# A macaron encoder layer in fp32: column updates ahead of the lower parts of X^T, the token scale spread one chunk later, and the first loads in another order

## The chip, the cores and the metric

The kernel runs on one core of a Trainium2 chip. The time is the device time of one execution in microseconds; 1860.35 us is the median of three runs (1859.88 to 1862.2). The engines are named as the profile names them: PE is the matrix engine and PEld its weight loads, DVE the vector engine, ACT the scalar engine, POOL the GpSimd engine, SP the engine whose queue issues nearly all loads.

## The reference

One layer on 256 tokens of width 2048, all in float32; the feed-forward width is 5632.

```python
ff = swiglu(rms_norm(x, pre_norm_ffn1), w_ffn1_gate_up, w_ffn1_down)
x = x + 0.5 * rms_norm(ff, post_norm_ffn1)
h = rms_norm(x, pre_norm_mix)
q_h, i_h, f_fwd, f_bwd, g_h, q_a, k_a, v_a = split(h @ w_mix_in)
y_h = hgrn2_mixer(q_h, i_h, f_fwd, f_bwd, g_h, ...)   # gated linear recurrence, both ways
y_a = window_attention(q_a, k_a, v_a, attn_sink, rel_bias_table)
x = x + rms_norm(concat(y_h, y_a) @ w_mix_out, post_norm_mix)
ff = swiglu(rms_norm(x, pre_norm_ffn2), w_ffn2_gate_up, w_ffn2_down)
x = x + 0.5 * rms_norm(ff, post_norm_ffn2)

def rms_norm(x, gain): return x * rsqrt(mean(x * x, -1) + 1e-6) * gain
def swiglu(x, w_gate_up, w_down):
    gate, up = split(x @ w_gate_up); return (silu(gate) * up) @ w_down
```

The change touches the first feed-forward block's start, the normalisation of both feed-forward blocks, and the ends of the first feed-forward block and of the mixer, where `x` is updated and the next product begins.

## The kernel before

**Products.** Every fp32 operand is a sum of two parts: `h`, the value rounded by a cast on ACT (L176), and `l`, the rest, by a subtraction on DVE (L177). A product is three matmuls of 128x512 on PE: h with X's upper part, l with X's upper part, h with X's lower part. Weights come in raw tiles of 128x2048 (three buffers, `raw`), each cast in two halves of 128x1024 into `h` and `l` (five buffers each). A raw tile is one unit of a group, and `work(u)` of a group is the products of one unit.

**X^T.** X lies in rows of 128 tokens (m = 0, 1) and four quarters of 512 columns (q = 0 to 3). `turn(m, q)` (L210) makes four transposes on PE into one bank, of the pool `pa` for m = 0 and `pb` for m = 1. `take_hi` (L227) makes the upper part on ACT, times a gain, and `take_lo` (L232) the lower part on DVE. A step in the code named T(m, q) below is `turned(m, q)`.

**The start** is written by hand (`manual_schedule`): the instructions of every engine stand in the order of the code. X^T of the first quarter, the first unit in pieces, then T(0,1), T(1,1) and the units 1 and 2, with `busy` matmuls of no use between the first ones. Group 0 of the gate/up product runs on the raw X^T, without the token scale 1/rms.

**The token scale.** While group 0 runs, the sums of squares are made on ACT, and at unit 4 the scale is spread over all partitions: two diagonal matrices `dg` on DVE (L267), a product with ones on PE (L268), a copy into `R` (L269). Then eight multiplications on DVE (`even`, L818) scale X^T in place, a few a unit, and all later groups read the scaled X^T. In the first block the bias rows of the attention are made beside it (`aside`, L1000 and L1001).

**The ends.** `finish` (L588 to L726) runs the last held units of the down (or output) product bank by bank: (m, n) = (0,0), (0,1), (1,0), (1,1). After each bank come the squares on ACT (L569) and the products with the gain on DVE (`gains`, L576); after n = 1 the row's factor `r` (tot, v, then a power on POOL, L182 to L186). `update(m, q)` (L623) adds `y * r` to a quarter of X, and T(m, q) turns that quarter for the next product, whose first two units are the *lead*: `lead.pieces(m)` yields four pieces of it, and `lead.more(i)` casts one half of its second unit. Order on PE, DVE and ACT is the order of the code here too; elsewhere a scheduler orders. The last `finish` (no gain) is another branch.

Of the kernel before, what the change touches and what calls it, by code (L numbers as in the profile page):

```python
# [37 lines left out]
def hymba_layer_kernel(  # L38
# [53 lines left out]
    def load_x(m, q, n=1):  # L92
        sl = slice(q * 512, (q + n) * 512)
        nc.sync.dma_start(res["X"][:, m, sl], x[0, m * P : (m + 1) * P, sl])
# [31 lines left out]
    def busy(n):  # L126

        bank = pb()
        for i in range(n):
            nc.tensor.matmul(bank, idle[:, 0:P], idle, start=(i == 0), stop=(i == n - 1))  # L130
# [98 lines left out]
    def take_lo(*a):  # L229

        for src, g, hi, lo in take_views(*a):
            nc.vector.scalar_tensor_tensor(  # L232
                lo, src, g, hi.bitcast(F32), ALU.mult, ALU.subtract
            )
# [275 lines left out]
    class Pairs(Blocks):  # L510
# [62 lines left out]
        def gains(self, m, n, dst=None):  # L573
            if dst is None:
                dst = self.y[m, 2 * self.now + n]
            nc.vector.tensor_tensor(  # L576
                dst, self.c[m][n], self.pg[:, n * 512 : (n + 1) * 512], ALU.mult
            )
# [9 lines left out]
        def finish(self, mul, post, new_x=None, gain=None, lead=None):  # L588


            order = self.orders[1]
            n_order = len(order)
            self.post = post
            self.work(n_order - self.HELD)
            held = []
            for u in order[n_order - self.HELD :]:
                held.append((u, *split_load(self.source(u), hp=post, lp=post)))
            close_far()
            self.half_gain(post)
            if new_x:  # L600
                new_x()
            X = res["X"]
            if lead:
                lead.load()
            r = [None, None]
            y = self.y

            def products(m, n, part):
                for u, k, hs, ls in [
                    (u, k, hs, ls) for u, hs, ls in held for k in range(2)  # L610
                ][part]:
                    self.plain(u, hs, ls, m, n, k)

            def squares(m, n):
                self.squares(m, n)
                if n == 1:
                    r[m] = rsqrt_of(self.ssq[m], 1.0 / (D * mul * mul), EPS / (mul * mul))

            gains = self.gains

            def update(m, q):
                sl = slice(q * 512, (q + 1) * 512)
                nc.vector.scalar_tensor_tensor(  # L623
                    X[:, m, sl], y[m, q], r[m], X[:, m, sl], ALU.mult, ALU.add
                )

            def update_aside(m, q):
                sl = slice(q * 512, (q + 1) * 512)
                nc.scalar.mul(y[m, q], y[m, q], r[m])
                nc.gpsimd.tensor_tensor(X[:, m, sl], X[:, m, sl], y[m, q], ALU.add)  # L630

            ordered = {mybir.EngineType.PE, mybir.EngineType.DVE, mybir.EngineType.Activation}
            every = slice(None)
            if gain is None:
                def store(m, q):
                    sl = slice(q * 512, (q + 1) * 512)
                    nc.sync.dma_start(out[0, m * P : (m + 1) * P, sl], X[:, m, sl])

                def in_place(n):
                    gains(1, n, dst=self.c[1][n])  # L640
                    y[1, 2 + n] = self.c[1][n]

                with tc.manual_schedule(engines=ordered):
                    products(0, 0, every)
                    squares(0, 0)
                    gains(0, 0)
                    products(0, 1, every)
                    squares(0, 1)
                    gains(0, 1)
                    products(1, 0, every)  # L650
                    squares(1, 0)
                    for q in range(4):
                        update(0, q)
                    in_place(0)
                    products(1, 1, every)
                    squares(1, 1)
                    in_place(1)
                    for q in range(4):
                        store(0, q)
                    update_aside(1, 0)  # L660
                    for q in (1, 2, 3):
                        update(1, q)
                        store(1, q)
                    store(1, 0)
                return None

            xt = new_xt()

            banks = {}

            def turned(m, q):
                banks[m, q] = turn(m, q)

            def hi(m, q):
                take_hi(m, q, gain, xt, banks[m, q])

            def lo(m, q):
                take_lo(m, q, gain, xt, banks[m, q])

            with tc.manual_schedule(engines=ordered):  # L680
                products(0, 0, every)
                squares(0, 0)
                gains(0, 0)
                products(0, 1, every)
                squares(0, 1)
                update(0, 0)
                gains(0, 1)
                products(1, 0, every)
                lead.more(0)
                update(0, 1)  # L690
                squares(1, 0)
                gains(1, 0)
                products(1, 1, slice(0, 3))

                def took(m, q):
                    hi(m, q)
                    lo(m, q)

                turned(0, 0)
                took(0, 0)  # L700
                products(1, 1, slice(3, None))
                turned(0, 1)
                squares(1, 1)
                took(0, 1)
                update(1, 0)
                update(1, 1)
                lead.more(1)
                first, second = lead.pieces(0, xt), lead.pieces(1, xt)
                next(first)
                next(first)  # L710
                turned(1, 0)
                took(1, 0)
                gains(1, 1)
                next(first)
                turned(1, 1)
                took(1, 1)
                for _ in first:
                    pass
                for m, q in ((0, 2), (1, 2), (0, 3), (1, 3)):
                    update(m, q)  # L720
                    next(second)
                    turned(m, q)
                    took(m, q)
                for _ in second:
                    pass
            return xt  # L726

# [66 lines left out]
    def ffn(gated, w_dn, post_gain, again, gain=None, lead=None, aside=None):  # L794

        with ExitStack() as st:
# [74 lines left out]
            for g in range(NG):  # L871
                if g:
                    gated.group(g)
                for u in range(gated.pos, KT // 2):
                    gated.work(u + 1)
                    if g == 0:
                        if u == 4:
                            power_and_rest()
                            spread(two)
                        for done in {4: (0, 1, 2), 5: (3, 4), 6: (5, 6), 7: (7,)}.get(u, ()):  # L880
                            even(done)
                        if u == 5 and aside:
                            aside()
                    if waiting and u == 0:
                        next(waiting)
                waiting = units(gated.c, rest if g else rs2)
                next(waiting)
# [26 lines left out]
    with tc.manual_schedule():  # L914
# [12 lines left out]
        def arrive(i):  # L927
            nc.sync.dma_start(raw[:, i * 512 : (i + 1) * 512], first[:, i // 2, i % 2])
# [5 lines left out]
        def half(i):  # L934
            cs = slice(i * 512, (i + 1) * 512)
            split_act(h[:, cs], l[:, cs], raw[:, cs])
# [6 lines left out]
        arrive(1)  # L943
        arrive(2)
        arrive(3)
        load_x(0, 1)
        load_x(1, 1)
        raws = [load(gated.source(1))]
        load_x(0, 2, 2)
        load_x(1, 2, 2)  # L950
        raws.append(load(gated.source(2)))
        turned(0, 0)
        taken(0, 0, [0])
        busy(3)
        half(0)
        taken(0, 0, [1, 2, 3])
        turned(1, 0)
        piece(0, 0)
        taken(1, 0, [0])
        half(1)  # L960
        piece(1, 0)
        piece(0, 1)
        piece(1, 1)
        hs, ls = zip((h, l), split_half(raw, 1))
        gated.parts = {0: (hs, ls)}
# [1 line left out]
        gated.piece(0, 1, 0)  # L967
        gated.piece(0, 1, 1)
        gated.parts[1] = split(raws[0])
        turned(0, 1)  # L970
        turned(1, 1)
        taken(0, 1)
        taken(1, 1)
        for k in range(2):
            for m in range(2):
                gated.piece(1, k, m)
        gated.parts[2] = split(raws[1])
        for k in range(2):
            for m in range(2):
# [505 lines left out]
```

## Time and profile before

| what | value |
|---|---|
| median of three runs | 1860.35 us |
| profiled execution, its own time | 1860.08 us |
| its span | 1858.2 us |
| PE busy | 1842.7 us, 99% |
| DVE busy | 1539.6 us, 83% |
| ACT busy | 1066.8 us, 57% |
| mean granted clock of PE | 0.999 |
| chain that ended last | PE 78%, DVE 14%, ACT 3%, issue 3%, DMA 1% |

The profiled execution is 1.9 us longer than its span, which begins and ends with the instructions of the trace. A matmul's record lasts about 0.39 us, and records of one engine overlap, so what a product costs is the step from one start to the next: about 0.227 us for 128x512. PE is not idle anywhere for more than 1.4 us at a time; the idle time lies at the start, at the two spreads and at the two ends.

### The profile page before, as it was taken

The page shows a single profiled execution, that of the slowest core. Times are in us where ns is not written, and L with a number is a line of the kernel's source. Part 1 is how long each engine was busy: PE and PEld are TensorE (multiplying, and loading weights), DVE is VectorE, ACT ScalarE, POOL GpSimd, SP SyncE. Part 2 cuts the span into 40 slices and gives each one's busy share as a digit, 9 for nine tenths or more (in the row PEclk, how much of TensorE's full clock was granted, in tenths as well). Part 3 has the DMA queues.
Part 4 walks back from the last instruction along what each step waited for, and adds up shares of the span by engine and source line. Part 5 has one row for each costly group of instructions (what it writes and reads, how often), then busy time and mean ns, then how long its engine had stood idle before and what let it go on. Part 6 is the DMA issues. An engine that isn't in the chain of part 4 may idle for free.

```text
span 1858.2 us, 23293 instructions
## 1 busy us (share of the span) xinstructions
PE 1842.7 (99%) x8682; PEld 1533.3 (83%) x8682; DVE 1539.6 (83%) x1932; ACT 1066.8 (57%) x1421; POOL 20.8 (1%) x39
## 2 busy tenths in 40 slices
PE   9999999999999999999999999999999999999998
PEld 6888888888887887888888887888888888887886
DVE  7978888888888888577787788888888888888887
ACT  6555555555555565577677655555554555555553
POOL 1000000000000000000000000000000000000000
PEclk9999999999999999999999999999999999999999
DMA  7665655555556465555565556565665556555464
GB/s 252 204 203 184 206 200 182 181 200 200 197 207 227 181 242 203 192 179 168 168 186 153 181 190 215 181 207 193 209 207 192 195 198 208 176 195 218 180 257 155
DMA packets 180881, 365.79 MB, mean 197 GB/s; under 512 B 9256, under 2 KB 56448, under 8 KB 180000
## 3 DMA queue, kind: packets, MB, share of 16 engines
q1 hardware_dynamic: 180416, 364.17, 56.9%
q8 instruction: 68, 1.11, 0.2%
q14 instruction: 45, 0.37, 0.1%
q0 software_dynamic: 352, 0.14, 0.0%
HBM read 360.06 MB, written 4.21 MB: 196 GB/s over the span
## 4 chain that ended last, share of the span: by engine, by line
PE 78%; DVE 14%; ACT 3%; issue 3%; DMA 1%; POOL 0%; ACTq 0%; SPq 0%; DVEq 0%; POOLq 0%
PE pa L420 30%; PE pb L420 29%; DVE l L177 8%; PE pa L299 8%; PE pa L304 4%; ACT h L176 2%; DVE raw L444 2%; DVE raw L450 1%; DVE raw L448 1%; DMA raw<-in_w_ffn_gate_up_dram 1%; DVE sp L177 1%; PE pa L354 1%; PE pa L352 1%; PE pa L353 1%; ACT xt L227 1%
## 5 line engine op out<-in xcount | busy, mean ns | idle before, releaser
L176 ACT CAST h<-raw 128x1024 fp32r<-128x1024 f32 (+1 forms) x825 | 807.5, 1009 | 669.6 <-PE pb L420 309.1
L177 DVE TENSOR_TENSOR l<-raw,h 128x1024 fp32r<-128x1024 f32 (+1 forms) x825 | 936.7, 1167 | 237.0 <-ACT h L176 203.8
L420 PE MATMUL pa<-h,xt 128*128 128x512 f32 x1248 | 431.2, 392 | 0.0
L420 PE MATMUL pb<-h,xt 128*128 128x512 f32 x1168 | 407.3, 390 | 0.0
L420 PEld LDWEIGHTS pa<-h,xt 128*128 128x128 f32 x1248 | 234.1, 188 | 48.7 <-ACT h L176 0.8
L420 PEld LDWEIGHTS pb<-h,xt 128*128 128x128 f32 x1168 | 219.2, 188 | 45.9 <-DVE xt L232 0.2
L420 PE MATMUL pa<-l,xt 128*128 128x512 f32 x624 | 243.2, 390 | 0.0
L420 PE MATMUL pb<-l,xt 128*128 128x512 f32 x584 | 227.3, 389 | 0.0
L420 PE MATMUL pa<-h,ht 128*128 128x512 f32 x560 | 193.4, 390 | 0.0
L420 PE MATMUL pb<-h,ht 128*128 128x512 f32 x488 | 171.8, 390 | 0.0
L299 PE MATMUL pa<-xt,h 128*128 128x512 f32 x672 | 164.7, 394 | 0.0
L299 PEld LDWEIGHTS pa<-xt,h 128*128 128x128 f32 x672 | 123.0, 188 | 23.6
L420 PEld LDWEIGHTS pa<-l,xt 128*128 128x128 f32 x624 | 117.2, 188 | 24.0 <-DVE l L177 0.6
L420 PEld LDWEIGHTS pb<-l,xt 128*128 128x128 f32 x584 | 109.7, 188 | 22.6
L420 PEld LDWEIGHTS pa<-h,ht 128*128 128x128 f32 x560 | 105.1, 188 | 22.4 <-DVE pa L487 0.5
L420 PE MATMUL pa<-l,ht 128*128 128x512 f32 x280 | 109.3, 390 | 0.0
L420 PEld LDWEIGHTS pb<-h,ht 128*128 128x128 f32 x488 | 91.6, 188 | 19.5 <-DVE pb L488 0.3
L444 DVE TENSOR_TENSOR raw<-raw 128x1024 f32<-128x1024 f32 x80 | 97.8, 1222 | 1.6
L420 PE MATMUL pb<-l,ht 128*128 128x512 f32 x244 | 95.0, 389 | 0.0
L304 PE MATMUL pa<-xt,l 128*128 128x256 f32 x672 | 91.5, 285 | 0.0
L304 PEld LDWEIGHTS pa<-xt,l 128*128 128x128 f32 x672 | 87.1, 191 | 3.2
L420 PEld LDWEIGHTS pa<-l,ht 128*128 128x128 f32 x280 | 52.6, 188 | 11.5 <-DVE l L177 0.7
(270 smaller groups left out, 1994.6 us busy)
## 6 DMA issues: line engine op xcount, KB each, us to landing
raw<-in_w_ffn_gate_up_dram SPq DMA_DIRECT2D x350, 512.0 KB, 4.8
raw<-in_w_ffn_down_dram SPq DMA_DIRECT2D x88, 1024.0 KB, 5.2
raw<-in_w_mix_in_dram SPq DMA_DIRECT2D x52, 1024.0 KB, 5.0
raw<-in_w_mix_out_dram SPq DMA_DIRECT2D x16, 1024.0 KB, 5.0
pg<-in_post_norm_ffn_dram SPq DMA_DIRECT2D x4, 512.0 KB, 5.7
X<-in_x_dram SPq DMA_DIRECT2D x2, 1024.0 KB, 5.9
bias<-row SPq DMA_DIRECT2D x16, 128.0 KB, 4.6
kept<-X SPq DMA_DIRECT2D x2, 1024.0 KB, 4.9
```

The source lines that it names most:

```text
L176: nc.scalar.copy(hi, src)
L177: nc.vector.tensor_tensor(lo, src, hi.bitcast(F32), ALU.subtract)
L227: last["act"] = nc.scalar.mul(hi, src, g)
L299: nc.tensor.matmul(slot[f], weights(hs, kk, f), xcol(xt, k), start=(k == 0), stop=(k == KT - 1))
L304: nc.tensor.matmul(slot[f][:, 0:T], weights(ls, kk, f), xcol(xt, kh * 8 + kk, 0), start=False, stop=False,)
L352: nc.tensor.matmul(dst, xh, h[:, o : o + n], start=(k == 0), stop=False)
L353: nc.tensor.matmul(dst, xh, l[:, o : o + n], start=False, stop=False)
L354: nc.tensor.matmul(dst, xl, h[:, o : o + n], start=False, stop=(k == KT - 1))
L420: nc.tensor.matmul(self.bank(at), lhs, rhs, start=(n == 1), stop=n in (ends, self.of[at]), skip_group_check=n > ends,)
L444: nc.vector.tensor_tensor(four[:, 0:2], four[:, 0::3], four[:, 1:2].to_broadcast([P, 2, 512]), ALU.add)
L448: nc.vector.tensor_tensor(b22, b11, b22, ALU.add)
L450: nc.vector.tensor_tensor(b21, b22, b21, ALU.add)
```

## The change

There are three parts. In `finish` with a gain, both halves of the lead's second unit are cast right behind `gains(0, 0)`; the updates of the last quarters, (0,2), (0,3), (1,2) and (1,3), stand ahead of the lower parts of X^T of the first quarters; the lower parts are made in pairs of blocks; three lead pieces stand ahead of T(1,0) instead of two. In `ffn` the spread comes at unit 5 instead of 4, and the eight multiplications by `R` at units 5, 6 and 7 (three, three, two) instead of 4 to 7 (three, two, two, one). In the start the second unit's load is issued ahead of X's second quarter and the third unit's ahead of its last two; `busy` is 2 instead of 3; pieces and halves of the first unit are interleaved otherwise; and T(0,1) and T(1,1) stand behind the halves of unit 1, with their upper and lower parts behind that.

```diff
@@ -674,54 +674,57 @@
             def hi(m, q):
                 take_hi(m, q, gain, xt, banks[m, q])
 
-            def lo(m, q):
-                take_lo(m, q, gain, xt, banks[m, q])
+            def lo(m, q, js=range(4)):
+                take_lo(m, q, gain, xt, banks[m, q], js)
 
             with tc.manual_schedule(engines=ordered):
                 products(0, 0, every)
                 squares(0, 0)
                 gains(0, 0)
+                lead.more(0)
+                lead.more(1)
                 products(0, 1, every)
                 squares(0, 1)
                 update(0, 0)
                 gains(0, 1)
                 products(1, 0, every)
-                lead.more(0)
                 update(0, 1)
                 squares(1, 0)
                 gains(1, 0)
+                update(0, 2)
+                update(0, 3)
                 products(1, 1, slice(0, 3))
-
-                def took(m, q):
+                turned(0, 0)
+                hi(0, 0)
+                products(1, 1, slice(3, None))
+                lo(0, 0, (0, 1))
+                turned(0, 1)
+                squares(1, 1)
+                hi(0, 1)
+                lo(0, 0, (2, 3))
+                lo(0, 1, (0, 1))
+                update(1, 0)
+                lo(0, 1, (2, 3))
+                update(1, 1)
+                first, second = lead.pieces(0, xt), lead.pieces(1, xt)
+                for _ in range(3):
+                    next(first)
+                turned(1, 0)
+                hi(1, 0)
+                next(first)
+                lo(1, 0)
+                turned(1, 1)
+                hi(1, 1)
+                gains(1, 1)
+                lo(1, 1)
+                update(1, 2)
+                update(1, 3)
+                for m, q in ((0, 2), (1, 2), (0, 3), (1, 3)):
+                    next(second)
+                    turned(m, q)
                     hi(m, q)
                     lo(m, q)
-
-                turned(0, 0)
-                took(0, 0)
-                products(1, 1, slice(3, None))
-                turned(0, 1)
-                squares(1, 1)
-                took(0, 1)
-                update(1, 0)
-                update(1, 1)
-                lead.more(1)
-                first, second = lead.pieces(0, xt), lead.pieces(1, xt)
-                next(first)
-                next(first)
-                turned(1, 0)
-                took(1, 0)
-                gains(1, 1)
-                next(first)
-                turned(1, 1)
-                took(1, 1)
-                for _ in first:
-                    pass
-                for m, q in ((0, 2), (1, 2), (0, 3), (1, 3)):
-                    update(m, q)
-                    next(second)
-                    turned(m, q)
-                    took(m, q)
-                for _ in second:
+                for _ in (*first, *second):
                     pass
             return xt
 
@@ -874,10 +877,10 @@
                 for u in range(gated.pos, KT // 2):
                     gated.work(u + 1)
                     if g == 0:
-                        if u == 4:
+                        if u == 5:
                             power_and_rest()
                             spread(two)
-                        for done in {4: (0, 1, 2), 5: (3, 4), 6: (5, 6), 7: (7,)}.get(u, ()):
+                        for done in {5: (0, 1, 2), 6: (3, 4, 5), 7: (6, 7)}.get(u, ()):
                             even(done)
                         if u == 5 and aside:
                             aside()
@@ -943,23 +946,23 @@
         arrive(1)
         arrive(2)
         arrive(3)
+        raws = [load(gated.source(1))]
         load_x(0, 1)
         load_x(1, 1)
-        raws = [load(gated.source(1))]
+        raws.append(load(gated.source(2)))
         load_x(0, 2, 2)
         load_x(1, 2, 2)
-        raws.append(load(gated.source(2)))
         turned(0, 0)
         taken(0, 0, [0])
-        busy(3)
         half(0)
+        busy(2)
+        piece(0, 0)
+        half(1)
         taken(0, 0, [1, 2, 3])
         turned(1, 0)
-        piece(0, 0)
         taken(1, 0, [0])
-        half(1)
+        piece(0, 1)
         piece(1, 0)
-        piece(0, 1)
         piece(1, 1)
         hs, ls = zip((h, l), split_half(raw, 1))
         gated.parts = {0: (hs, ls)}
@@ -967,13 +970,13 @@
         gated.piece(0, 1, 0)
         gated.piece(0, 1, 1)
         gated.parts[1] = split(raws[0])
-        turned(0, 1)
-        turned(1, 1)
-        taken(0, 1)
-        taken(1, 1)
         for k in range(2):
             for m in range(2):
                 gated.piece(1, k, m)
+                if m:
+                    turned(0, 1) if k == 0 else turned(1, 1)
+        taken(0, 1)
+        taken(1, 1)
         gated.parts[2] = split(raws[1])
         for k in range(2):
             for m in range(2):
```

In the rows of order below, a name's number after the underscore only tells buffers apart and differs between the two kernels. On PE, in the start, the last product of unit 0, both transposes and the first of unit 1 stood like this before:

```order
L420 MATMUL pb_119<-l_186,xt_123 128x512
L420 MATMUL pb_119<-h_185,xt_123 128x512
L210 MATMUL pa_215<-ident,X_75 128x128 x4
L210 MATMUL pb_220<-ident,X_75 128x128 x4
L420 MATMUL pa_116<-h_207,xt_123 128x512
L420 MATMUL pa_116<-l_208,xt_123 128x512
```

and now the end of unit 1's first half, T(0,1), the end of its second half, T(1,1) (`pb_243`) and the first products of unit 2 (`h_264`, `l_265`) stand like this:

```order
L420 MATMUL pb_119<-h_206,xt_123 128x512
L210 MATMUL pa_226<-ident,X_75 128x128 x4
L420 MATMUL pa_116<-h_210,xt_123 128x512
```

```order
L420 MATMUL pb_119<-l_211,xt_123 128x512
L420 MATMUL pb_119<-h_210,xt_123 128x512
L210 MATMUL pb_243<-ident,X_75 128x128 x4
L420 MATMUL pa_116<-h_264,xt_123 128x512
L420 MATMUL pa_116<-l_265,xt_123 128x512
L420 MATMUL pa_116<-h_264,xt_123 128x512
```

Both groups of transposes have moved behind products of unit 1; T(1,1) is now the last thing on PE ahead of unit 2. On ACT in the same place, before (`h_207`, `h_211` are unit 1, `h_265` is unit 2):

```order
L227 ACTIVATE xt_123<-pb_164,gain_102 128x128 x3
L176 CAST h_207<-raw_137 128x1024
L176 CAST h_211<-raw_137 128x1024
L227 ACTIVATE xt_123<-pa_215,gain_102 128x128 x4
L227 ACTIVATE xt_123<-pb_220,gain_102 128x128 x4
L176 CAST h_265<-raw_142 128x1024
L176 CAST h_269<-raw_142 128x1024
```

and now (`h_206`, `h_210` are unit 1, `h_264` is unit 2):

```order
L227 ACTIVATE xt_123<-pb_168,gain_102 128x128 x3
L176 CAST h_206<-raw_135 128x1024
L176 CAST h_210<-raw_135 128x1024
L227 ACTIVATE xt_123<-pa_226,gain_102 128x128 x4
L227 ACTIVATE xt_123<-pb_243,gain_102 128x128 x4
L176 CAST h_264<-raw_140 128x1024
L176 CAST h_268<-raw_140 128x1024
```

The kinds stand in the same sequence: the upper parts of `pa` and `pb`, which read T(0,1) and T(1,1), are ahead of unit 2's first cast. The same holds on DVE for the lower parts and `l_265`.

On DVE behind the first spread (`R` from `pb`), before (`l_640` is the first l of group 1):

```order
L818 TENSOR_TENSOR xt_124<-xt_124,R 128x1024
L177 TENSOR_TENSOR xs_482<-s_478,xs_482 128x4x128
L824 TENSOR_TENSOR z_522<-xt_124 128x512
L818 TENSOR_TENSOR xt_124<-xt_124,R 128x1024
L380 TENSOR_TENSOR s_524<-z_522 128x256
L177 TENSOR_TENSOR l_598<-raw_590,h_597 128x1024
L383 TENSOR_TENSOR s_524<-s_524,z_522 128x128
L177 TENSOR_TENSOR l_640<-raw_636,h_639 128x1024
```

and now (`l_639` is the first l of group 1; `l_592` and `l_596`, the last of group 0, stand ahead of R):

```order
L821 TENSOR_TENSOR xt_124<-xt_124,R 128x1024
L384 TENSOR_TENSOR s_512<-z_510,s_512 128x128
L821 TENSOR_TENSOR xt_124<-xt_124,R 128x1024
L177 TENSOR_TENSOR xs_516<-s_512,xs_516 128x4x128
L827 TENSOR_TENSOR z_578<-xt_124 128x512
L821 TENSOR_TENSOR xt_124<-xt_124,R 128x1024
L380 TENSOR_TENSOR s_580<-z_578 128x256
L821 TENSOR_TENSOR xt_124<-xt_124,R 128x1024
L383 TENSOR_TENSOR s_580<-s_580,z_578 128x128
L177 TENSOR_TENSOR l_639<-raw_635,h_638 128x1024
```

All eight multiplications by R are now ahead of group 1's first l; before, one was behind it, and an l of group 0 stood between them.

On ACT in the end of the first feed-forward block, before (the casts of `raw_5781` are the lead's second unit, `raw_6104` the unit behind the lead):

```order
L569 ACTIVATE jk_5810,ssqr_4050<-pa_4952 128x512
L569 ACTIVATE jk_5825,ssqr_4050<-pa_4953 128x512
L176 CAST h_5847<-raw_5781 128x1024
L569 ACTIVATE jk_5852,ssqr_4051<-pb_4954 128x512
L227 ACTIVATE xt_5794<-pa_5864,cols 128x128 x4
L569 ACTIVATE jk_5885,ssqr_4051<-pb_4955 128x512
L227 ACTIVATE xt_5794<-pa_5880,cols 128x128 x4
L176 CAST h_5903<-raw_5781 128x1024
L176 CAST h_6106<-raw_6104 128x1024
```

and now (`raw_5780` is the lead's second unit, `raw_6103` the unit behind the lead):

```order
L569 ACTIVATE jk_5809,ssqr_4049<-pa_4951 128x512
L176 CAST h_5812<-raw_5780 128x1024
L176 CAST h_5816<-raw_5780 128x1024
L176 CAST h_6105<-raw_6103 128x1024
L569 ACTIVATE jk_5832,ssqr_4049<-pa_4952 128x512
L569 ACTIVATE jk_5855,ssqr_4050<-pb_4953 128x512
L227 ACTIVATE xt_5793<-pa_5869,cols 128x128 x4
L569 ACTIVATE jk_5888,ssqr_4050<-pb_4954 128x512
L227 ACTIVATE xt_5793<-pa_5883,cols 128x128 x4
```

Three casts have moved between the squares of (0,0) and those of (0,1), the third of them of the unit behind the lead.

## Rows read from the trace of the kernel before

**Rows 1.** The page: busy time of each engine.
```profile
PE 1842.7 (99%) x8682; PEld 1533.3 (83%) x8682; DVE 1539.6 (83%) x1932; ACT 1066.8 (57%) x1421; POOL 20.8 (1%) x39
```

**Rows 2.** Waits of PE: us in total, times, longest.
```profile
PE pb L268 <- DVE dg L267: 1.8, 2, 1.0
PE pa L210 <- DVE X L623: 1.5, 2, 1.2
PE pb L210 <- DVE X L623: 0.9, 2, 0.5
```

**Rows 3.** Timeline, PE, start: start us, us, line, operation [idle before].
```profile
3.84 1.03 PE L130 MATMUL pb<-idle 128*128 128x512 bf16 x2
...
7.20 0.84 PE L210 MATMUL pb<-ident,X 128*128 128x128 f32 x4
7.80 0.48 PE L420 MATMUL pa<-h,xt 128*128 128x512 f32 x1
...
13.86 0.60 PE L210 MATMUL pa<-ident,X 128*128 128x128 f32 x4
14.30 0.60 PE L210 MATMUL pb<-ident,X 128*128 128x128 f32 x4
...
20.20 0.39 PE L420 MATMUL pa<-h,xt 128*128 128x512 f32 x1
20.43 0.39 PE L420 MATMUL pa<-l,xt 128*128 128x512 f32 x1
```

**Rows 4.** Timeline, ACT, start.
```profile
8.35 1.56 ACT L176 CAST h<-raw 128x512 fp32r<-128x512 f32 x2
...
14.50 1.14 ACT L227 ACTIVATE xt<-pa,gain 128x128 fp32r<-128x128 f32 x4 [0.25 <-PE pa L210]
15.51 1.16 ACT L227 ACTIVATE xt<-pb,gain 128x128 fp32r<-128x128 f32 x4
17.12 1.05 ACT L176 CAST h<-raw 128x1024 fp32r<-128x1024 f32 x1 [0.45 <-DMA raw<-in_w_ffn_gate_up_dram]
```

**Rows 5.** Timeline, DVE, start.
```profile
18.20 1.23 DVE L177 TENSOR_TENSOR l<-raw,h 128x1024 fp32r<-128x1024 f32 x1 [0.37 <-ACT h L176]
```

**Rows 6.** Timeline, PE, at the first spread of the token scale.
```profile
38.88 0.39 PE L420 MATMUL pa<-h,xt 128*128 128x512 f32 x1
40.30 0.71 PE L268 MATMUL pb<-dg,ones 128*128 128x128 f32 x4 [1.03 <-DVE dg L267]
...
45.74 1.02 PE L1000 MATMUL pb<-bias_rows,tab 32*8 32x512 f32 x2
...
46.78 0.47 PE L420 MATMUL pa<-h,xt 128*128 128x512 f32 x1
```

**Rows 7.** Timeline, DVE, behind that spread.
```profile
41.49 0.42 DVE L269 COPY R<-pb 128x256 f32<-128x256 f32 x1
41.94 4.63 DVE L818 TENSOR_TENSOR xt<-xt,R 128x1024 fp32r<-128x1024 f32 x4
46.49 0.68 DVE L824 TENSOR_TENSOR z<-xt 128x512 f32<-128x512 f32 x1
...
55.45 1.22 DVE L177 TENSOR_TENSOR l<-raw,h 128x1024 fp32r<-128x1024 f32 x1
```

**Rows 8.** Timeline, PE, end of the first feed-forward block.
```profile
718.37 0.60 PE L210 MATMUL pa<-ident,X 128*128 128x128 f32 x4
...
737.31 0.66 PE L210 MATMUL pa<-ident,X 128*128 128x128 f32 x4 [1.20 <-DVE X L623]
```

**Rows 9.** Timeline, ACT, in that end.
```profile
713.86 0.60 ACT L569 ACTIVATE jk<-pa 128x512 bf16<-128x512 f32 x1 [2.09 <-PE pa L420]
```

**Rows 10.** Timeline, DVE, in that end.
```profile
715.61 0.75 DVE L623 SCALAR_TENSOR_TENSOR X<-y,r,X 128x512 f32<-128x512 f32 x1 [0.69 <-POOL r L186]
```

**Rows 11.** DMA issued from 708.4 to 709: KB, us from issue to landing.
```profile
raw<-in_w_mix_in_dram SPq DMA_DIRECT2D x1, 1024.0 KB, 6.4
```

**Rows 12.** Windows: busy us (instructions) of each engine, PEclk, DMA share, GB/s.
```profile
720.00:740.00 20.00, 17.97 (x85) 13.45 (x85) 17.28 (x41) 12.99 (x33) 1.02 (x2) 1.00 0.34 108
```

## The prediction

> **What bounds the kernel now.** I read the page first: PE is busy for 99% of the span [rows 1], so the forecast is about single waits of PE. The view of waits names those the change aims at: the token scale's spread on PE waits twice for `dg`, 1.8 us in all, and the transposes four times for an update of X, 1.5 and 0.9 us [rows 2]. Both sums together are 4.2 us, 0.23% of the time. The timelines then show what each engine does around these places, and the order of the changed kernel what will stand there. A product steps by 0.23 (20.20 to 20.43), and a group of four transposes costs 0.44 (13.86 to 14.30) [rows 3]. A consumer on ACT follows a group's start by 0.64: the transposes at 13.86 [rows 3] are read at 14.50 [rows 4].
>
> **The start: +3.7.** The change moves T(0,1) and T(1,1) behind products of unit 1. Before, the two groups stood at 13.86 and 14.30 [rows 3], six microseconds and 24 products ahead of unit 2, and ACT and DVE made X^T's parts under those products. Now T(1,1) is the last thing on PE ahead of unit 2, while on ACT its four upper parts stay ahead of unit 2's first cast. Stepped through:
> - First unit: T(1,0) stood at 7.20, ahead of the first product at 7.80 [rows 3]; now three products stand ahead of it. ACT's long cast, in the records from 8.35 [rows 4], then starts about 0.34 later (my stepping), so unit 1 begins not at 13.86 but at about 14.20.
> - T(1,1) starts at 14.20 + 24 x 0.227 + 0.44 = 20.09. ACT begins its upper parts 0.64 later, 20.73, needs 1.01 for four (14.50 to 15.51), and casts unit 2 for 1.05 [rows 4]: 21.74 to 22.79.
> - DVE subtracts for 1.23, beginning 0.03 after the cast's end (17.12 + 1.05 = 18.17, then 18.20) [rows 4, 5]: 22.82 to 24.05. PE's first l product of unit 2 starts at about 24.1, against 20.43 before [rows 3].
>
> That is 3.7, with nothing else to do for PE: the waiting h products stand at the head of its queue, and l products right behind. The loads moved up (unit 1's and unit 2's ahead of X's quarters) don't help, since unit 2 now waits for a cast that is queued, not for its load; before, that cast came on its load at 17.12 [rows 4] and still had three microseconds. Bounds: 0 if the cast gets ahead of the upper parts, and 4.2 if leaving out one `busy` matmul, two of which last 1.03 at 3.84 [rows 3], lets PE reach its full pace that much later.
>
> The Trainium skill, in "TensorE: Matmul & The Clock Gate", Part 1, says ScalarE and VectorE take their instructions strictly first in, first out. Rows 4 and 5 agree, as each cast there starts only behind the upper parts ahead of it; were it otherwise, this term would be near 0.
>
> **The first spread: -1.2 and +2.0.** The wait of 1.03 for `dg` at 40.30 goes; with the restart it is 40.30 - 38.88 - 0.23 = 1.19 [rows 6]. One unit, 24 products or 5.4 us, covers it. But the multiplications by R move later by that unit, while group 1 stays. Call P the start of the spread's product on PE. R's copy starts at P + 0.75 (the product's record of 0.71 [rows 6] and 0.04 to the consumer). From there to the end of group 1's first l, DVE has by the order: R 0.45 (41.49 to 41.94); eight multiplications at 1.14 (four from 41.94 to 46.49); four operations of 0.60 (0.68 less an overlap of 0.08, as 1.22 steps by 1.14), the aside's bias rows among them; the aside's columns and five short sums, about 0.24 each; the l itself 1.22 [rows 7]. That is 0.45 + 9.12 + 2.40 + 1.42 + 1.22 = 14.6, so the l ends at P + 15.4. PE reaches group 1 after the spread and the aside (0.46 + 1.04, the latter 46.78 - 45.74 [rows 6]) and two units of 24 products, P + 12.5, and has four h products ahead of the first l: it wants it at P + 13.4. So it waits 2.0. Before, this l began at 55.45 [rows 7], ended at 56.7, and PE came to it at 58.0: a slack of 1.3, which the move of a unit, 5.4, spends, though the l of group 0 that stood between is now ahead of R. The last multiplication must also wait for unit 7's last product (about P + 12.7), which is when DVE gets to it: no extra cost. Bounds: 0 and 3.
>
> **The end of the first block: -1.2.** The updates (0,2) to (1,3) now stand ahead, so the transposes' waits go: 1.20 at 737.31 [rows 8], 0.30 and 0.48 of the same kind, 1.98 in all (in the sums of 1.5 for `pa`, and of 0.9 for `pb` with the mixer's 0.46 [rows 2]). In those 20 us PE is idle for 2.03 by the records [rows 12], and restarts hide about as much again in steps over 0.23: some 3.2. New waits come in. ACT has three casts between the squares of (0,0) and (0,1), the third from a weight tile that lands 6.4 after its issue at about 708.5 [rows 11], at 714.9. The cast ends at 715.96, and squares(0,1), at 713.86 before [rows 9], start 2.1 later; on DVE the l of the same tile stands ahead of `tot` too, 0.5 more. So update(0,0) moves from 715.61 [rows 10] to 718.2 and ends near 719.0, where its transposes want it at 718.37 [rows 8]: +0.6. T(0,1) follows an update that is as late: +0.8; the first lower parts stand behind four updates: +0.55. 2.0 against 3.2 is -1.2. Bounds -2.5 and +0.6.
>
> **The mixer's end: -0.2.** There the same tile has landed long before; update (0,0) is later by its casts alone and its transposes don't wait. 0.46 of a wait goes [rows 2], with its restart and short gaps 1.2, and about 1.0 comes for lower parts behind the updates (0,2), (0,3).
>
> **The second spread: -0.4.** 0.76 of the 1.8 [rows 2] goes, 0.92 with its restart. No aside stands here, and one multiplication stays behind group 1's first l: that l ends at P + 11.7 where it is wanted at P + 11.6, the second at P + 15.6 against 15.2: 0.1 and 0.4 come back.
>
> **Sum.** 3.7 - 1.2 + 2.0 - 1.2 - 0.2 - 0.4 = +2.7; a slack of 0.1 remains in other small gaps of group 1, so +2.6. The profiled execution took 1860.08, which is 0.27 under the runs' median of 1860.35; 1862.7 by the one, 1862.9 by the other. I say 1862.7. About 0.2%, 3.7 us, is what a measurement of this kernel tells from no change, so this is "same" on its slower side.
>
> **Rivals.**
> - *PE's clock falls in the start's wait (slower).* In the first microseconds PE runs at half pace: four transposes last 0.84 at 7.20 and 0.60 at 13.86 [rows 3], though the granted clock reads 1.00; that is the lower of the two levels, 1.2 against 2.4 GHz, and it rose after steady work. In the new wait PE idles for about 2.1 and, four products later, 0.85. If it falls for as long as at the start, some 6 us, half of that is lost: +3.0, 1865.7. For it: idle work stands at the start to raise it, and one `busy` less is left. Against: after 1.20 idle at 737.31 [rows 8] it did not fall. It decides when the step after 24.1 is 0.43. The Trainium skill, in the same Part 1, says that the throttled state is the default and activity releases it, and warns of idle gaps; no row here shows a gap of 2.1 in the middle. Chance 0.2.
> - *The start doesn't wait.* If the cast runs under T(1,1)'s products after all, 3.4 of the 3.7 goes: 1859.3. Against it the order on ACT. Chance 0.15.
> - *All waits go and nothing takes their place.* -1.2 - 0.9 - 3.2 - 1.2 = -6.5: 1853.6. It needs the start, the l behind R and ACT's casts all to be harmless. Chance 0.1.
>
> **How the numbers follow.** The forecast has 0.55, own range 1860.5 to 1864.9 (the spread's 0 to 3, the end's bounds). The range reaches from 1857.0, half way to "all waits go", to 1866.5, the clock's case with the spread's upper bound. Faster than 1856.6: 0.1 and a little of the second rival, 0.13. Slower than 1864.1: the clock's case, 0.2, and a fifth of the forecast, 0.1: 0.3. The rest 0.57.
>
> **What would show it.** Right: PE idle for about 2 us at 20.7 released by ACT's cast of unit 2, then by DVE's l; no wait for `dg`; a wait of 2 us for a DVE l near 63 us; squares(0,1) at about 716; no wait near 737. Wrong: unit 2's products at 20.5, which would take the largest term away, or steps of 0.43 behind it.

## The result and the profile after

The changed kernel takes 1865.37 us (median of ten runs, 1863.42 to 1867.59) against 1860.42 (ten runs): a ratio of 1.0025, 95% interval 1.0015 to 1.0035. It is slower by 5 us (0.25%, clear of the noise, though far below 2%); 1862.7 was forecast. Its runs spread over 4 us. The profiled execution took 1865.95 and its span is 1864.1. All ratios below are to the kernel before, measured again beside each run (1860.1 to 1860.2).

The waits of PE after (us in total, times, longest):

```profile
PE pa L420 <- ACT h L176: 2.7, 2, 2.2
PE pa L420 <- DVE l L177: 2.6, 3, 1.7
PE pb L130 <- DVE idle L124: 1.4, 1, 1.4
PE pa L354 <- DVE xt L232: 1.1, 1, 1.1
PE pa L420 <- DVE xt L232: 0.9, 1, 0.9
```

No wait for `dg` or for an update of X [rows 2] is in the list any more; waits for casts, for `l` and for X^T's lower part stand in their place.

To see where time came and went, take the start of the nth 128x512 product in either trace, counted from 0; both have 7344 of them. A step in the difference marks the place, so long as both orders have done the same work there (at product 47 they have not quite: T(1,1), about 0.36, is still to come in the new order):

```
product  before   after   difference
47        19.98   20.30     +0.32   last of unit 1
49        20.43   24.66     +4.23   first l product of unit 2
72        27.41   34.26     +6.85   first of unit 3
150       48.24   53.76     +5.52   behind the first spread
300       83.16   91.16     +8.00   in group 1
3150     747.87  754.33     +6.46   behind the end of the first block
4600    1215.46 1221.36     +5.90   behind the mixer's end and the second spread
6650    1689.31 1695.24     +5.93
```

**The start.** PE after (start us, us, operation, idle before):

```profile
20.54 0.60 PE L210 MATMUL pb<-ident,X 128*128 128x128 f32 x4
23.30 0.80 PE L420 MATMUL pa<-h,xt 128*128 128x512 f32 x1 [2.17 <-ACT h L176]
24.66 0.80 PE L420 MATMUL pa<-l,xt 128*128 128x512 f32 x1 [0.57 <-DVE l L177]
...
26.11 0.63 PE L420 MATMUL pa<-l,xt 128*128 128x512 f32 x1
26.53 0.63 PE L420 MATMUL pa<-h,xt 128*128 128x512 f32 x1
26.96 1.06 PE L210 MATMUL pa<-ident,X 128*128 128x128 f32 x4
...
30.24 0.60 PE L210 MATMUL pb<-ident,X 128*128 128x128 f32 x4
```

then ACT and DVE:

```profile
21.17 1.14 ACT L227 ACTIVATE xt<-pb,gain 128x128 fp32r<-128x128 f32 x4 [2.07 <-PE pb L210]
22.19 4.85 ACT L176 CAST h<-raw 128x1024 fp32r<-128x1024 f32 x5
```

```profile
22.35 1.13 DVE L232 SCALAR_TENSOR_TENSOR xt<-pb,gain,xt 128x128 fp32r<-128x128 f32 x4 [2.09 <-ACT xt L227]
23.39 4.62 DVE L177 TENSOR_TENSOR l<-raw,h 128x1024 fp32r<-128x1024 f32 x4
```

T(1,1) is read 0.63 after its start; four upper parts take 1.02; only then comes unit 2's cast, with ACT idle for 2.07 before all that. This is the chain that the forecast stepped through, 0.45 later in time. On DVE the same order holds `l` back: it begins at 23.39, right behind the lower parts of T(1,1). Behind the wait a product's record lasts 0.63 to 0.80 and four transposes 1.06, where they last 0.39 and 0.60 at 30.24 and later, and at 13.86 before [rows 3]. The windows after (busy us of PE, PEld, DVE, ACT, POOL; granted clock; DMA share, GB/s) say why:

```profile
20.00:24.00 4.00, 1.83 (x9) 1.01 (x7) 1.91 (x7) 2.83 (x6) 0.00 (x0) 0.91 0.76 280
24.00:28.00 4.00, 3.43 (x11) 2.77 (x11) 4.00 (x4) 3.03 (x4) 0.00 (x0) 0.50 0.20 50
28.00:32.00 4.00, 4.00 (x17) 3.19 (x16) 2.27 (x6) 2.70 (x8) 1.04 (x2) 0.74 0.64 237
```

The granted clock is 0.50, the lower of the two levels, from about 23.3 (0.91 over four microseconds leaves 0.7 of them at half) to 30.1 (0.74 leaves 2.1). It fell at the end of the 2.17 in which PE was idle, and twelve of unit 2's 24 products ran at it.

**The spreads.** After, the spread's product at 50.72 follows the product ahead of it without a gap; then PE waits for group 1's first l, which ends at 66.06:

```profile
50.72 0.60 PE L268 MATMUL pb<-dg,ones 128*128 128x128 f32 x4
...
66.11 0.50 PE L420 MATMUL pa<-l,xt 128*128 128x512 f32 x1 [1.75 <-DVE l L177]
```

```profile
51.36 0.42 DVE L269 COPY R<-pb 128x256 f32<-128x256 f32 x1 [0.85 <-PE pb L268]
...
63.50 1.23 DVE L821 TENSOR_TENSOR xt<-xt,R 128x1024 fp32r<-128x1024 f32 x1
64.64 0.28 DVE L383 TENSOR_TENSOR s<-s,z 128x128 f32<-128x128 f32 x1
64.84 1.22 DVE L177 TENSOR_TENSOR l<-raw,h 128x1024 fp32r<-128x1024 f32 x1
```

The l ends at P + 15.3 with P = 50.72; the forecast said P + 15.4. From R's copy to that l's begin DVE takes 13.5 now (51.36 to 64.84) and took 14.0 before (41.49 to 55.45 [rows 7]). So DVE takes no longer there: R comes one unit later, and group 1 doesn't.

**The end of the first block.** On ACT and DVE after:

```profile
722.53 1.05 ACT L176 CAST h<-raw 128x1024 fp32r<-128x1024 f32 x1 [0.82 <-DMA raw<-in_w_mix_in_dram]
723.49 0.59 ACT L569 ACTIVATE jk<-pa 128x512 bf16<-128x512 f32 x1
```

```profile
725.78 0.75 DVE L623 SCALAR_TENSOR_TENSOR X<-y,r,X 128x512 f32<-128x512 f32 x1 [0.69 <-POOL r L186]
```

The squares of (0,1) stand behind a cast that waits for its load, as stepped through from [rows 9 to 11]. By the shift of 8.0 on PE, the update at 725.78 is 2.2 later than 715.61 [rows 10]. The wait of 1.20 [rows 8] was that of T(0,3), which now stands at 741.36 without one; a wait for X^T's lower part has come in:

```profile
726.59 0.66 PE L210 MATMUL pa<-ident,X 128*128 128x128 f32 x4
...
730.03 0.50 PE L354 MATMUL pa<-h,xt 128*128 128x512 f32 x1 [1.06 <-DVE xt L232]
...
741.36 0.60 PE L210 MATMUL pa<-ident,X 128*128 128x128 f32 x4
```

### The profile page after: what moved, and what is told of

It reads as the page before. It is cut to its first block, busy times and chain, and to the rows that moved or that the text cites. A ratio compares the mean times of both kernels' runs of the same rounds, so it can differ in the third digit from the quotient of the medians.

```text
span 1864.1 us, 23303 instructions
## 1 busy us (share of the span) xinstructions
PE 1845.1 (99%) x8681; PEld 1535.3 (82%) x8681; DVE 1538.8 (83%) x1932; ACT 1066.1 (57%) x1421; POOL 23.3 (1%) x39
## 4 chain that ended last, share of the span: by engine, by line
PE 77%; DVE 17%; issue 3%; ACT 2%; DMA 1%; POOL 0%; SPq 0%; ACTq 0%; DVEq 0%; POOLq 0%
PE pa L420 30%; PE pb L420 28%; DVE l L177 10%; PE pa L299 8%; PE pa L304 4%; ACT h L176 2%; DVE raw L444 2%; DVE raw L450 1%; DVE raw L448 1%; PE pa L354 1%; PE pa L353 1%; PE pa L352 1%; DVE sp L177 1%; DVE xt L821 1%; PE pa L856 0%
```

## The experiments

The theory: the start costs a wait of some 4 us, because unit 2's cast is queued on ACT behind the upper parts of T(1,1), and 2.5 to 3 more, because PE's clock falls in that wait; the spread costs about 1; the ends gain about 2. Rivals: the clock falls for another reason; the load, not the queue, makes unit 2 late; the l behind the spread is late only since DVE is behind from the start.

**The new start alone**: of the change's diff only the part behind `arrive(3)`, in the kernel before.

> The kernel before with the new start alone. If the start costs what the two traces show at the 100th product (6.85 us: 3.8 of waiting for unit 2's cast and l, 3.0 of products at the lower clock), the time is about 1867.2 and the trace shows the same wait of 2.2 at 20.7 and a granted clock of 0.50 behind it. If the clock's fall needs something of the other parts, the wait alone remains: about 1864.2. If the start is harmless by itself: 1860.4.

Measured 1864.89 (1863.44 to 1868.11), ratio 1.0027 (1.0017 to 1.0038). The wait of 2.2 and the clock's fall are both there without the other parts:

```profile
22.54 0.50 PE L420 MATMUL pa<-h,xt 128*128 128x512 f32 x1 [2.16 <-ACT h L176]
23.90 0.50 PE L420 MATMUL pa<-l,xt 128*128 128x512 f32 x1 [0.86 <-DVE l L177]
```

```profile
20.00:24.00 4.00, 0.98 (x6) 0.42 (x4) 2.42 (x6) 3.59 (x7) 0.00 (x0) 1.00 0.70 258
24.00:28.00 4.00, 4.00 (x14) 3.22 (x15) 3.60 (x5) 3.41 (x7) 0.46 (x1) 0.61 0.36 107
28.00:32.00 4.00, 4.00 (x22) 3.31 (x21) 3.01 (x8) 3.04 (x9) 0.58 (x2) 0.96 0.64 180
```

The cost at product 72 is 5.2, not 6.85: unit 1 ends 0.44 earlier than before here, where it was 0.32 later in the changed kernel's execution (and up to 0.92 later in the others with this start), and the clock was low for less long: granted 0.61 in 24 to 28 and 0.96 in 28 to 32, so 3.4 us and not 6.8. Here it fell only behind the second wait. The changed kernel's one execution over-stated the start's cost; the mechanism holds.

**The old start** in the changed kernel: the same part of the diff undone.

> The changed kernel with the old start. If the parts add up: 1860.4 - 1.3 (no wait for dg) + 2.5 (wait for group 1's first l and what follows) - 1.5 (end of the first block) - 0.5 (mixer's end and second spread) = 1859.6, with the clock at 1.00 everywhere. If the l's wait was there only because DVE was behind from the start, it goes as well: 1857.1.

Measured 1859.66 (1859.22 to 1860.58), ratio 0.9999 (0.9990 to 1.0007): the sum of the parts. The start is the whole of the loss: the other two parts together change nothing that the interval can tell. The wait for group 1's first l stays at 1.7, so it does not come from the start.

**Idle matmuls in the wait.**

```diff
+        busy(9)
         taken(0, 1)
         taken(1, 1)
```

> The changed kernel with nine idle matmuls on PE behind T(1,1), where it waits. If the idle stretch is what lowers the clock, the granted clock stays at 1.00, the wait of unit 2 stays (its first product at about 23.3, first l at 24.7), and the time falls by 3.0 to 1862.4. If the clock falls for another reason (the idle matmul left out at the start, or the short waits before 10 us), it still falls: 1865.4 or a little more.

Measured 1863.19 (1862.15 to 1863.95), ratio 1.0016 (1.0007 to 1.0025). PE, and the windows:

```profile
21.09 0.60 PE L210 MATMUL pb<-ident,X 128*128 128x128 f32 x4
21.74 1.89 PE L130 MATMUL pb<-idle 128*128 128x512 bf16 x8
23.85 0.49 PE L420 MATMUL pa<-h,xt 128*128 128x512 f32 x1 [0.22 <-ACT h L176]
25.21 0.50 PE L420 MATMUL pa<-l,xt 128*128 128x512 f32 x1 [0.87 <-DVE l L177]
```

```profile
20.00:24.00 4.00, 3.73 (x19) 2.20 (x18) 1.93 (x9) 2.27 (x6) 0.00 (x0) 1.00 0.72 264
24.00:28.00 4.00, 3.13 (x15) 2.38 (x16) 4.00 (x5) 4.00 (x7) 0.00 (x0) 1.00 0.07 12
```

The trace has eight of the nine. Work of no use makes the changed kernel faster by 2.2, where 3.0 was expected: unit 2 is held back as long, 4.03 from product 47 (0.88 late) to product 72 (4.91), T(1,1) included, but the clock stays at 1.00. In the changed kernel the same stretch cost 6.53, so the clock's fall cost 2.5 in that execution, and 2.2 between the medians. What lowers it is the idle stretch and not the `busy` matmul left out earlier, which is left out here too.

**Unit 2's casts ahead of the parts of T(1,1).**

```diff
         taken(0, 1)
-        taken(1, 1)
         gated.parts[2] = split(raws[1])
+        taken(1, 1)
```

> The changed kernel with unit 2's casts ahead of the parts of T(1,1) on ACT and DVE; nothing else moves in the code. If the queue order on ACT is what makes PE wait, unit 2's first product follows T(1,1) at about 20.9, the clock stays, and 6.5 us go: 1858.9. If the parts of T(1,1) are then late for unit 2's second half (m = 1), about 1 us of it comes back: 1860. If unit 2's load was the limit after all, the wait stays: 1865.4.

Measured 1860.79 (1860.21 to 1861.53), ratio 1.0003 (0.9994 to 1.0012). PE:

```profile
21.13 0.60 PE L210 MATMUL pb<-ident,X 128*128 128x128 f32 x4
21.48 0.48 PE L420 MATMUL pa<-h,xt 128*128 128x512 f32 x1
22.06 0.50 PE L420 MATMUL pa<-l,xt 128*128 128x512 f32 x1
...
24.59 0.73 PE L420 MATMUL pb<-h,xt 128*128 128x512 f32 x2 [0.20 <-DVE xt L232]
```

The queue's order is the cause, not the load: unit 2 follows T(1,1) at once, and the granted clock reads 1.00 from 20 to 32. The edit moves the cast on ACT and `l` on DVE together; how much each of the two queues holds back alone was not tried. The second half's wait is 0.2. The time is 1.9 above the expected 1858.9: unit 1 ends 0.92 later than before in this execution, not 0.32, and T(1,1) itself with short waits up to product 72 (2.23 late there) adds 1.3. The profiled execution, 1861.53, is also the slowest of its eleven.

**The new spread alone**: `u == 5` and its table of multiplications, in the kernel before.

> The kernel before with the spread one unit later alone. From the same run: first block -1.5 for dg and +2.5 for group 1's first l and what follows, second block -1.0 and +0.9, so about +0.9: 1861.1. If the l's wait comes from something else than the multiplications ahead of it on DVE, only the gains remain: 1857.7.

Measured 1861.60 (1860.83 to 1864.72), ratio 1.0010 (1.0001 to 1.0018): a small loss by itself, its interval barely clear of 1; product 4600 is 1.22 late in its trace. Both waits for `dg` go, at the second spread too, and the l's wait of 1.75 comes with an undisturbed start.

**The new ends alone**: the diff's part in `finish`, in the kernel before.

> The kernel before with the new ends alone. In the run with the old start the two ends gave -1.3 and -0.1 by the products' start times, so 1858.8, with a wait for X^T's lower part of about 1.1 in the first block's end (behind the updates (0,2) and (0,3)) in place of the waits for updates. If the gain needs the later spread, nothing: 1860.2.

Measured 1857.45 (1856.88 to 1859.66), ratio 0.9987 (0.9978 to 0.9995). Better than the parts' sum by 1.35. The second spread's wait for `dg`, 0.76 before, is gone although the spread stays at unit 4: PE's waits of this kernel list `dg` once, in the first block:

```profile
PE pa L354 <- DVE xt L232: 1.1, 1, 1.1
PE pb L268 <- DVE dg L267: 0.9, 1, 0.9
PE pa L420 <- DVE xt L232: 0.8, 1, 0.8
```

The updates of the last quarters come earlier, and so do the squares that `dg` waits for: ACT's last of them starts at 1161.71, where before it is 1169.53. So beside the new ends the later spread buys nothing at the second place, and still costs: in the changed kernel 0.84 goes there between products 4445 and 4600.

**The last multiplications behind group 1's first l**, with the old start.

```diff
-  for done in {5: (0, 1, 2), 6: (3, 4, 5), 7: (6, 7)}.get(u, ()):
+  for done in {5: (0, 1, 2), 6: (3, 4), 7: (5,)}.get(u, ()):
...
+  if g == 1 and u == 0:
+      even(6)
+      even(7)
```

> The changed kernel with the old start, and the last two multiplications by R moved to the first unit of group 1, behind its l on DVE. If the multiplications ahead of that l are the cause of the wait, it ends 2.3 earlier (two of 1.14), the 2.0 at group 1's begin goes, and most of the 0.9 in the second block: 1859.66 - 2.5 - 0.5 = 1856.7. If DVE is then late with l's further on, the time stays at 1859.7.

Measured 1859.75 (1859.26 to 1860.21), ratio 0.9998 (0.9989 to 1.0007): nothing gained. The wait at group 1's begin (at 59.07 with the old start) is gone, but waits come some 13 us later:

```profile
72.07 0.50 PE L420 MATMUL pa<-l,xs 128*128 128x512 f32 x1 [0.72 <-DVE l L177]
...
73.75 0.50 PE L420 MATMUL pb<-h,xs 128*128 128x512 f32 x1 [0.49 <-ACT h L176]
...
74.70 0.73 PE L420 MATMUL pa<-h,xt 128*128 128x512 f32 x2 [0.21 <-ACT h L176]
```

DVE had no slack there: in the kernel before it is busy for 19.5 of 20 us twice in a row (the third number behind the comma, 19.45 and 19.46):

```profile
40.00:60.00 20.00, 19.70 (x86) 15.45 (x87) 19.45 (x28) 7.83 (x10) 0.55 (x1) 1.00 0.49 158
60.00:80.00 20.00, 20.00 (x94) 16.62 (x94) 19.46 (x24) 10.39 (x13) 0.00 (x0) 1.00 0.61 206
```

Work moved there by one unit, 5.4 us, was paid for at the one place or the other.

**The updates (0,2) and (0,3) behind the lower parts**, on top of that.

```diff
-                update(0, 2)
-                update(0, 3)
                 products(1, 1, slice(0, 3))
...
                 lo(0, 1, (2, 3))
                 update(1, 1)
+                update(0, 2)
+                update(0, 3)
```

> As the run before, and the updates (0,2) and (0,3) moved behind the lower parts of T(0,0), T(0,1) and update (1,1), into a stretch of 2.3 us in which DVE waits for ACT. If those two updates are what makes the first lower part late, the waits for it go (1.2 with restart in the first block's end, 0.9 in the mixer's end): 1854.7. If the quarter (0,2) is then late for its transposes, part of that comes back: 1855 to 1857.

Measured 1857.63 (1857.20 to 1858.40), ratio 0.9986 (0.9977 to 0.9995): 2.1 below the run before, as the move should give; the expected 1854.7 carried the 3 us that the run before did not gain.

**The same ends with the old start and the old spread.**

> The kernel before (old start, old spread) with the new ends, and in them the updates (0,2) and (0,3) behind the lower parts of T(0,0) and T(0,1) and update (1,1). The run with the new ends alone took 1857.45 and has waits of 1.1 and 0.8 for a lower part of X^T; in the best run so far that move took such waits away and gave 2.1 there. So 1855.4. If the gain of the ends in the second spread (its wait for dg was gone) hangs on the earlier updates, 1 us comes back: 1856.4.

Measured 1855.61 (1854.96 to 1856.27), ratio 0.9976 (0.9966 to 0.9985): the fastest version, 4.6 below the kernel before. The second wait for `dg` stays away.

**The lead's casts behind the squares of (0,1).**

```diff
                 gains(0, 0)
-                lead.more(0)
-                lead.more(1)
...
                 gains(0, 1)
+                lead.more(0)
                 products(1, 0, every)
                 update(0, 1)
+                lead.more(1)
```

> The same, with the casts of the lead's second unit behind the squares of (0,1) and of (1,0) instead of ahead of the squares of (0,1). If the three casts ahead of those squares are what makes T(0,0) wait (0.5 us), it goes: 1854.9. If the squares of (1,0) are then late in the same way, update (1,0) is late and T(1,0) waits: 1855.4 or more.

Measured 1857.75 (1857.57 to 1858.73), ratio 0.9988 (0.9979 to 0.9997): 2.1 worse than with the casts ahead. The edit is not quite what the expectation says: `lead.more(1)` stands ahead of the squares of (1,0), which follow it in the code. T(0,0) indeed waits no more, but the lead's l parts now stand on DVE ahead of X^T's first lower parts, whose waits grow to 1.4 at each end:

```profile
PE pa L354 <- DVE xt L232: 1.4, 1, 1.4
...
PE pa L420 <- DVE xt L232: 1.4, 1, 1.4
```

So putting both casts early was worth more than the 0.5 that it costs at T(0,0).

## Why the prediction came out as it did

The measured 1865.37 is above the 1860.5 to 1864.9 that the forecast gave for itself, and 0.3 below the 1865.7 of its rival on the clock. It lies in the wide range because that rival was counted in. So the terms of the sum held, and the sum lacked one.

- **The start's wait: right, a little small.** Forecast 3.7 at unit 2's first l product, from T(1,1), four upper parts, a cast and a subtraction in a row. Measured 4.23 there (24.66 against 20.43). The largest part of the difference is that unit 1 began at 14.60 and not at 14.20; in the profiled executions with this start it began between 13.83 and 15.21. `l` also waited for the lower parts on DVE, which the forecast left out. Only one h product, not four, stands between the two waits, which costs nothing. That rows 4 and 5 show ACT holding the cast back was read too freely, since the cast at 17.12 came on its load; the run with the cast put first shows it.
- **The clock: the rival that was given 0.2 is what happened.** The forecast took a wait of 2.1 as probably harmless because 1.20 idle at 737.31 [rows 8] had not lowered it; that row doesn't bear so far. It fell in the profiled executions of the changed kernel and of the new start alone, and the sign that the forecast named, steps of 0.43, is there (26.11 to 26.53). Its price was put at 3.0; 2.5 was measured in the profiled executions and 2.2 between the medians. This term, left out of the sum, is the largest part of what separates 1862.7 from 1865.4. How long the clock stays low differs between executions: the changed kernel's mean granted clock goes from 0.998 at 1863.42 to 0.995 at 1867.59, so at least part of the spread of its runs goes with it. The Trainium skill, in "TensorE: Matmul & The Clock Gate", Part 1, says that activity releases a throttled default; the fill with idle matmuls agrees, 1.00 against 0.50.
- **The first spread: right.** -1.33 measured (6.85 to 5.52) for -1.2, and +2.03 for +2.0; a further 0.45 of short waits in group 1 was not seen.
- **The end of the first block: right in sign and place, its parts wrong.** -1.54 for -1.2. The wait for X^T's lower part was 1.23 by PE's steps where 0.55 was put, but T(0,0) waited 0.2 and T(0,1) hardly, where 0.6 and 0.8 were put. The tile's load was issued as late as the products (716.56, before 708.51), but it landed 5.9 after its issue and not 6.4, so the cast, the squares and the update came 0.4 to 0.5 earlier than put. And the 0.8 counted again the 0.6 for which T(0,0) would already have waited: update (0,1), two DVE steps of 0.67 and 0.60 behind update (0,0) at 718.2, ends at about 720.2, and T(0,1) stood at 719.50 before. That the net still came within 0.4 is in part luck.
- **The mixer's end and the second spread: right in sum, -0.56 for -0.6, in part by luck.** Of the -0.56, 0.16 came inside the mixer, at a place that the change doesn't touch. At the second spread 1.02 went and 0.84 came back, where 0.92 and 0.5 were put. The gain of `dg` was booked to the later spread; the later spread alone brings it, and so do the ends alone, so the two can't be added.

By these steps, 0.32 + 3.91 + 2.62 - 1.33 + 2.48 - 1.54 - 0.53 = 5.93, against 5.87 between the two profiled executions; the third term is the lower clock with what else lies between products 49 and 72 (0.13 in the run with idle matmuls).

## What to carry to other kernels

When work on PE is moved later to fill a place, look at what reads its result on the other engines: what stands behind that reader in their queues is held up with it, however early its own data came. Here a wait of PE cost its length and, after 2.17 us of idling, also slower products behind it. Where such a wait can't be removed, try cheap matmuls in it: here they gave back 2.2 us. DVE, busy for 97% of its stretch, had no room for work "a little later". And measure the parts of a change alone: here one of the three carried all the gain.

## What the runs showed of the hardware

The granted clock fell to 0.50 at the end of 2.17 us of idle PE and stayed there for 6.8 us, through twelve products and four transposes; the products' steps were 0.43 where others are 0.23. With the new start alone it fell only behind the second wait, of 0.86, and for 3.4 us. It did not fall where idle matmuls filled that wait and left 0.22 and 0.87, nor after 1.20 at 737.31 before. The idle matmuls made the changed kernel faster by 2.2 us.
